# Residual stream kept token-major in a two-layer decoder trunk: down, w_out and wo with stationary activations, norms taken per token tile ahead of transposes

## The chip, the cores and the metric

One core of one Trainium2 chip runs the whole trunk. TensorE (PE) does the matmuls and its weight loads (PEld) run beside them; VectorE (DVE), ScalarE (ACT) and GpSimd (POOL) do the elementwise work; SyncE (SP) issues nearly all DMAs. Each engine works through its own list of instructions in a fixed order that a scheduler made when the kernel was built. The metric is device time in microseconds, from the first to the last instruction of the core plus what lies around them.

## The reference

512 tokens, width 1024, two layers, all in float32:

```python
for l in range(2):
    x = x + 0.5 * swiglu_ffn(rmsnorm(x, ffn1_norm[l]), gate, up, down)      # 1024 -> 2816 -> 1024
    z = rmsnorm(x, mix_norm[l]) @ w_in[l]                                    # 384 | 256 | 384 | 384 columns
    y = concat(s5(z_ssm), pool(z_pool), conv_module(z_v, z_g))
    x = x + y @ w_out[l]
    x = x + cross_attention(rmsnorm(x, xattn_norm[l]), rmsnorm(mem, mem_norm[l]), wq, wk, wv, wo)
    x = x + 0.5 * swiglu_ffn(rmsnorm(x, ffn2_norm[l]), gate, up, down)
return rmsnorm(x, final_norm)
```

rmsnorm(x, g) is x * rsqrt(mean(x^2) + 1e-6) * g. The conv module is v * sigmoid(g), a causal depthwise convolution of 31 taps, a layer norm over its 384 channels, and silu.

## The kernel before

**Layout.** The residual stream is feature-major: eight tiles `xs[k]` of 128 features by 512 tokens. Every projection has its weights stationary (128 x 128) and the activations of all 512 tokens moving, so its output is feature-major again. x is transposed on PE when it is loaded, and once more in the last FFN, whose last block is computed with stationary activations to give token-major output rows.

**Precision.** Weights and activations are split into two float32r parts, and `mm3` (L236 to L238) does three passes for each product. `wload` fetches a weight tile (L225), ACT makes the high part (L227), DVE or POOL the low part (L229); pools of three buffers stage them.

**Norms.** `Norm.add(k)` is called as soon as feature tile k of the residual stream is final: it splits x times gain, not yet divided by the root mean square, into `xh` and `xl`, and adds up squares. The next projections start on these at once. Meanwhile 4 matmuls against ones sum the squares over features (`ss_`, L202), DVE, POOL and PE turn that into a row factor that is broadcast over partitions (`pb_`, L214, copied to `rb` on ACT), and each projection multiplies by `rb` when its PSUM tile is evacuated on DVE: L269 and L273 in the FFN, L569, L572, L585 and L602 in the mixer, L853 in the attention.

**FFN.** 22 blocks of 128 hidden features; `gate_up(f)` makes one, and `down(p)` folds a group of six or five into the stream, eight output tiles each. `bg` is background work of the first phases (parameters, the memory's norm, the S5 matrices `s5_build`).

**Mixer.** In the order of PE: `pool_in` (`pp`), `conv_in(0)` (`pv`, `pgt`), `ssm_in` (`psu`), the other `conv_in`, then the keys and values of the memory (`kps`, `vps`), the S5 scan (`sps`, `yps`, `gps`) and w_out (`po`). On DVE stand the scaled memory `mg` (L800), the gated conv input `ch` (L569 to L573), the S5 input `su` (L585), then 3 x 29 multiply-adds of the convolution (`cacc`, L727) with S5 steps (`sy`, `sys`) between them, and the sum `lsm` that starts the layer norm (`lmean`, L740). The first half of w_out fills PE while the layer norm runs.

**Attention.** Per head: `q_proj` (`qps`), `scores`, softmax, and one head later `out_head` (`pv_`). After the last `out_head`, `wo` is applied to all eight feature tiles (`pwo`).

**Tail.** `finish` computes the last block token tile by token tile: residual add (L320), squares with an accumulator (L322), mean (L326), power on POOL (L327), scaling (L332, L334) and the output DMA.

Of the kernel before, what the change touches and what calls it, by code (L numbers as in the profile page):

```python
# [17 lines left out]
P = 128  # L18
# [26 lines left out]
def trunk_kernel(ctx: ExitStack, tc: tile.TileContext, io, out, phases=None):  # L45
# [30 lines left out]
    bp = ctx.enter_context(tc.tile_pool(name="bp", bufs=36))  # L76
# [86 lines left out]
    load_vecs(0)  # L163

# [6 lines left out]
    class Norm:  # L171
        def __init__(self, name, col, sum_eng=V):
            self.name, self.col, self.sum_eng = name, col, sum_eng
            self.xg = [None] * NK
            self.acc = None

        def sums(self, kt):
            sq = bt(f"sq_{self.name}{kt}")
            A.activation(out=sq, in_=xs[kt], func=AF.Square)
            if self.acc is None:  # L180
                self.acc = sq
            else:
# [10 lines left out]
        def r4(self):  # L193
            return rsqrt_cols(self.acc, 1.0 / D, self.name)
# [60 lines left out]
    def ffn(which, l, norm, nxt, bg):  # L255
# [22 lines left out]
        def down(p):  # L278
            f0, n = starts[p], sizes[p]
            last = p == len(sizes) - 1  # L280
            for o in range(NK):
# [3 lines left out]
                if last:  # L285
                    nxt.add(o)
# [736 lines left out]
```

## Time and profile before

| | |
|---|---|
| median of 3 runs | 2139.57 us (2138.98 to 2139.76) |
| span of the profiled execution | 2138.3 us |
| median less that span | 1.3 us |
| PE busy | 2088.5 us, 98% of the span |
| PEld busy | 1733.4 us, 81% |
| DVE busy | 1301.8 us, 61% |
| ACT busy | 751.5 us, 35% |
| POOL busy | 441.7 us, 21% |
| DMA queue q1, share of 16 engines | 33.8% |

The time of the profiled execution itself was not listed, so its span stands for it; the median lies 1.3 us above that span. A share is an average over the whole program: what a stage is worth is read from its own windows.

### The profile page before, as it was taken

The page shows a single profiled execution, that of the slowest core. Times are in us where ns is not written, and L with a number is a line of the kernel's source. Part 1 is how long each engine was busy: PE and PEld are TensorE (multiplying, and loading weights), DVE is VectorE, ACT ScalarE, POOL GpSimd, SP SyncE. Part 2 cuts the span into 40 slices and gives each one's busy share as a digit, 9 for nine tenths or more (in the row PEclk, how much of TensorE's full clock was granted, in tenths as well). Part 3 has the DMA queues.
Part 4 walks back from the last instruction along what each step waited for, and adds up shares of the span by engine and source line. Part 5 has one row for each costly group of instructions (what it writes and reads, how often), then busy time and mean ns, then how long its engine had stood idle before and what let it go on. Part 6 is the DMA issues. An engine that isn't in the chain of part 4 may idle for free.

```text
span 2138.3 us, 25180 instructions
## 1 busy us (share of the span) xinstructions
PE 2088.5 (98%) x9685; PEld 1733.4 (81%) x9685; DVE 1301.8 (61%) x1942; ACT 751.5 (35%) x1060; POOL 441.7 (21%) x477
## 2 busy tenths in 40 slices
PE   8999999989999999999999999999989999999998
PEld 6888888877787888888887888887868878888887
DVE  7766454699755544444577564456996655454454
ACT  4423222434434322222352323233344443222232
POOL 2217170457000000000013680006550000000000
PEclk9999999989999999999999999999999999999999
DMA  5342332444322323333333333334443323333241
GB/s 168 98 125 75 115 98 73 133 125 132 98 80 58 91 85 112 88 94 105 89 95 93 104 96 99 103 89 128 125 124 89 89 59 94 94 96 101 80 147 40
DMA packets 396256, 213.03 MB, mean 100 GB/s; under 512 B 31934, under 2 KB 387048, under 8 KB 396136
## 3 DMA queue, kind: packets, MB, share of 16 engines
q1 hardware_dynamic: 395344, 210.32, 33.8%
q8 instruction: 76, 1.25, 0.3%
q10 hardware_dynamic: 792, 1.10, 0.1%
q14 instruction: 44, 0.36, 0.1%
HBM read 203.32 MB, written 6.29 MB: 98 GB/s over the span
## 4 chain that ended last, share of the span: by engine, by line
PE 86%; DVE 10%; issue 1%; DMA 1%; ACT 1%; SPq 0%; POOL 0%; POOLq 0%; DVEq 0%; ACTq 0%
PE pgffn L236 7%; PE pgffn L237 7%; PE pgffn L238 7%; PE puffn L237 7%; PE puffn L238 7%; PE puffn L236 7%; PE pdffn L238 7%; PE pdffn L236 7%; PE pdffn L237 7%; DVE cacc L727 3%; PE qps L237 1%; PE po L236 1%; PE qps L236 1%; PE po L238 1%; PE pwo L236 1%
## 5 line engine op out<-in xcount | busy, mean ns | idle before, releaser
L236 PE MATMUL pgffn<-xh_ffn,wh_gffn 128*128 128x512 f32 x696 | 272.6, 392 | 0.0
L237 PE MATMUL puffn<-xl_ffn,wh_uffn 128*128 128x512 f32 x696 | 272.2, 391 | 0.0
L238 PE MATMUL puffn<-xh_ffn,wl_uffn 128*128 128x512 f32 x696 | 271.9, 391 | 0.0
L236 PE MATMUL puffn<-xh_ffn,wh_uffn 128*128 128x512 f32 x696 | 271.6, 390 | 0.0
L237 PE MATMUL pgffn<-xl_ffn,wh_gffn 128*128 128x512 f32 x696 | 271.4, 390 | 0.0
L238 PE MATMUL pgffn<-xh_ffn,wl_gffn 128*128 128x512 f32 x696 | 271.3, 390 | 0.0
L238 PE MATMUL pdffn<-h_ffffn,wl_dffn 128*128 128x512 f32 x664 | 257.9, 389 | 0.9 <-DVE wl_dffn L229 0.9
L237 PE MATMUL pdffn<-l_ffffn,wh_dffn 128*128 128x512 f32 x664 | 258.3, 389 | 0.0
L236 PE MATMUL pdffn<-h_ffffn,wh_dffn 128*128 128x512 f32 x664 | 257.8, 389 | 0.0
L227 ACT ACTIVATE wh_dffn<-wr_dffn 128x768 fp32r<-128x768 f32 (+1 forms) x120 | 94.9, 795 | 286.9 <-PE pdffn L237 148.3
L284 DVE SCALAR_TENSOR_TENSOR x<-pdffn,x 128x512 f32<-128x512 f32 x120 | 82.4, 689 | 168.7 <-PE pdffn L238 168.6
L273 DVE TENSOR_TENSOR uffn<-puffn,rb_ffn 128x512 f32<-128x512 f32 x88 | 60.7, 690 | 197.8 <-PE puffn L238 197.8
L227 ACT ACTIVATE wh_uffn<-wr_uffn 128x1024 fp32r<-128x1024 f32 x87 | 92.2, 1060 | 250.7 <-PE pgffn L237 155.2
L227 ACT ACTIVATE wh_gffn<-wr_gffn 128x1024 fp32r<-128x1024 f32 x87 | 92.2, 1060 | 249.5 <-issue 154.7
L269 DVE TENSOR_TENSOR affn<-pgffn,rb_ffn 128x512 f32<-128x512 f32 x88 | 60.7, 690 | 164.8 <-PE pgffn L238 158.6
L236 PEld LDWEIGHTS puffn<-xh_ffn,wh_uffn 128*128 128x128 f32 x696 | 131.0, 188 | 27.4 <-issue 0.2
L237 PEld LDWEIGHTS puffn<-xl_ffn,wh_uffn 128*128 128x128 f32 x696 | 131.0, 188 | 27.5 <-issue 0.2
L238 PEld LDWEIGHTS puffn<-xh_ffn,wl_uffn 128*128 128x128 f32 x696 | 131.0, 188 | 27.0
L238 PEld LDWEIGHTS pgffn<-xh_ffn,wl_gffn 128*128 128x128 f32 x696 | 130.7, 188 | 27.3
L237 PEld LDWEIGHTS pgffn<-xl_ffn,wh_gffn 128*128 128x128 f32 x696 | 130.8, 188 | 26.6
L236 PEld LDWEIGHTS pgffn<-xh_ffn,wh_gffn 128*128 128x128 f32 x696 | 130.7, 188 | 26.5
L238 PEld LDWEIGHTS pdffn<-h_ffffn,wl_dffn 128*128 128x128 f32 x664 | 124.6, 188 | 27.2 <-DVE wl_dffn L229 1.3
(456 smaller groups left out, 4197.4 us busy)
## 6 DMA issues: line engine op xcount, KB each, us to landing
wr_gffn<-in_ffn_w_gate_dram SPq DMA_DIRECT2D x87, 512.0 KB
wr_uffn<-in_ffn_w_up_dram SPq DMA_DIRECT2D x87, 512.0 KB
wr_dffn<-in_ffn_w_down_dram SPq DMA_DIRECT2D x64, 384.0 KB
wr_dffn<-in_ffn_w_down_dram SPq DMA_DIRECT2D x56, 320.0 KB
wr_k<-in_xattn_wk_dram SPq DMA_DIRECT2D x16, 512.0 KB
wr_v<-in_xattn_wv_dram SPq DMA_DIRECT2D x16, 512.0 KB
wr_wo<-in_w_out_dram SPq DMA_DIRECT2D x16, 512.0 KB
wr_q<-in_xattn_wq_dram SPq DMA_DIRECT2D x16, 512.0 KB
```

The source lines that it names most:

```text
L227: A.activation(out=h, in_=raw, func=AF.Copy)
L236: T.matmul(ps, lhsT=wh, rhs=ah, start=first, stop=False)
L237: T.matmul(ps, lhsT=wh, rhs=al, start=False, stop=False)
L238: T.matmul(ps, lhsT=wl, rhs=ah, start=False, stop=last)
L269: V.tensor_tensor(out=a, in0=pg, in1=rb, op=MUL)
L273: V.tensor_tensor(out=u, in0=pu, in1=rb, op=MUL)
L284: V.scalar_tensor_tensor(out=xs[o], in0=ps, scalar=0.5, in1=xs[o], op0=MUL, op1=ADD)
L727: V.scalar_tensor_tensor(out=acc[:, d:], in0=h[:, 0:S - d], scalar=cw[:, TAPS - 1 - d:TAPS - d], in1=acc[:, d:], op0=MUL, op1=ADD)
```

## The change

The residual stream becomes four token tiles `xt[t]` of 128 tokens by 1024 features, loaded by plain row DMAs. `down`, w_out and wo swap operands: 128 x 128 pieces of the activations are stationary, and rows of the weight matrix, 512 columns at a time, are moving, so their output is token-major and is added to `xt` by `add_x`. Each norm works per token tile: `Norm.half` squares each half (ACT, with an accumulator), and after the second half DVE, POOL and DVE make the normalised row tile `xn` with the gain, which is loaded broadcast over all partitions (`gb`); 8 PE transposes bring it feature-major, ACT copies `xh` and DVE makes `xl`. The projections then need no row factor. The first projection after a norm goes through `proj_halves`, two passes over 256 tokens each, so that its first half needs only token tiles 0 and 1. The FFN groups become 6, 6, 6, 4, and the last group's weight rows are kept in SBUF so that `finish` goes token tile by token tile in every FFN; w_out and wo do the same with their last three and two row blocks. Some evacuations go to ACT (`su`, `pd`), sigmoids read PSUM directly, and the first pass of wo (three heads) is placed ahead of the last head's `out_head`.

```diff
     class Norm:
...
+        def half(self, t, h):
...
+            A.activation(out=sq, in_=xt[t][:, dsl(h)], func=AF.Square, scale=D ** -0.5, accum_out=ss[:, h:h + 1])
+            if h == 1:
+                V.tensor_scalar(out=ss[:, 2:3], in0=ss[:, 0:1], scalar1=ss[:, 1:2], scalar2=EPS, op0=ADD, op1=ADD)
+                G.tensor_tensor(out=ss[:, 3:4], in0=ss[:, 2:3], in1=nhalf[:, 0:1], op=ALU.pow)
+                for i in range(2):
+                    self.emit(t, i, ss[:, 3:4])
+
+        def emit(self, t, h, r):
+            xn = bt(f"xn_{self.name}{t}{h}")
+            V.scalar_tensor_tensor(out=xn, in0=xt[t][:, dsl(h)], scalar=r, in1=self.gb[h], op0=MUL, op1=MUL)
+            ps = ax(f"xp_{self.name}{t}{h}", (P, NK // 2, P))
+            for k in range(NK // 2):
+                T.transpose(ps[:, k, :], xn[:, k * P:(k + 1) * P], ident)
+            A.activation(out=self.hl[0][h][:, :, tsl(t)], in_=ps, func=AF.Copy)
+            V.tensor_tensor(out=self.hl[1][h][:, :, tsl(t)], in0=ps, in1=self.hl[0][h][:, :, tsl(t)].bitcast(F32), op=SUB)
...
+    def proj_halves(items, acts):
+
+        n = len(acts)
+        for c in range(2):
+            cs = slice(c * S // 2, (c + 1) * S // 2)
+            for ps, (h, lo) in items:
+                for k, (ah, al) in enumerate(acts):
+                    mm3(ps[:, cs], h[:, k, :], lo[:, k, :], ah[:, cs], al[:, cs], c == 0 and k == 0, k == n - 1, True)
+
+
+    def rows_pass(dst, w, k0, acts, dh, name, first, last, eng=None, marks=None):
...
+            with tc.issue_after(marks[j // 2]) if marks else nullcontext():
+                for t, ps in dst:
+                    for i in range(m):
+                        ah, al = acts[j + i]
+                        mm3(ps, ah[:, tsl(t)], al[:, tsl(t)], got[j + i][0], got[j + i][1], first and j + i == 0,
+                            last and j + i == n - 1)
+        return got
...
+        def finish():
             for t in range(NT):
...
+                for dh in range(2):
+                    ps = mm(f"pl{which}{l}_{t}{dh}")
+                    rows_kept(ps, t, [gs[fl + i] for i in range(nl)], [kept[i][dh] for i in range(nl)], True, True)
+                    add_x(t, dh, ps, 0.5)
+                    nxt.half(t, dh)
...
-            a = vt(f"ca{l}_{i}")
-            V.tensor_tensor(out=a, in0=pgt, in1=rb, op=MUL)
-            A.activation(out=a, in_=a, func=AF.Sigmoid)
             h = vt(f"ch{l}_{i}")
-            V.tensor_tensor(out=h, in0=pv, in1=rb, op=MUL)
-            V.tensor_tensor(out=h, in0=h, in1=a, op=MUL)
+            A.activation(out=h, in_=pgt, func=AF.Sigmoid)
+            V.tensor_tensor(out=h, in0=pv, in1=h, op=MUL)
...
-            V.tensor_tensor(out=u, in0=pu.rearrange("p (c j) -> p j c", j=CH), in1=rbp, op=MUL)
+            A.activation(out=u, in_=pu.rearrange("p (c j) -> p j c", j=CH), func=AF.Copy)
...
+        n1 = (NH - 1) * HD // P
+        first = {(t, 0): (mm if t < 3 else cx)(f"pwo{l}_{t}0") for t in range(NT)}
+        rows_pass([(t, first[t, 0]) for t in range(NT)], wo, 0, os_[:n1], 0, f"xo{l}", True, False)
         out_head(NH - 1)
```

On DVE, the start of the convolution in layer 0's mixer reads as follows before the change: `mg` are the eight low parts of the scaled memory, `ca` and `ch` the gate and the value of conv tile 0, `su` the S5 input.

```order
L800 SCALAR_TENSOR_TENSOR mg_3_3493<-mn_1_3488,pcols_322,mg_3_3493 128x256
L569 TENSOR_TENSOR ca_0_3474<-pgt_0_3443,rb_mix_3344 128x512
L572 TENSOR_TENSOR ch_0_3477<-pv_0_3412,rb_mix_3344 128x512
L573 TENSOR_TENSOR ch_0_3477<-ch_0_3477,ca_0_3474 128x512
L800 SCALAR_TENSOR_TENSOR mg_4_3498<-mn_2_3496,pcols_322,mg_4_3498 128x256
L800 SCALAR_TENSOR_TENSOR mg_5_3501<-mn_2_3496,pcols_322,mg_5_3501 128x256
L727 SCALAR_TENSOR_TENSOR cacc_0_4464<-ch_0_3477,convw,cacc_0_4464 128x510
L727 SCALAR_TENSOR_TENSOR cacc_0_4464<-ch_0_3477,convw,cacc_0_4464 128x509
L800 SCALAR_TENSOR_TENSOR mg_6_3506<-mn_3_3504,pcols_322,mg_6_3506 128x256
L800 SCALAR_TENSOR_TENSOR mg_7_3509<-mn_3_3504,pcols_322,mg_7_3509 128x256
L727 SCALAR_TENSOR_TENSOR cacc_0_4464<-ch_0_3477,convw,cacc_0_4464 128x508
L585 TENSOR_TENSOR su_0_3583<-psu_0_3552,rb_mix_3344 128x512
```

The same place on DVE after the change (`pq` is the pooled mean of pool tile 0, whose sums `pw` POOL makes):

```order
L801 SCALAR_TENSOR_TENSOR mg_4_3471<-mn_2_3469,pcols_344,mg_4_3471 128x256
L801 SCALAR_TENSOR_TENSOR mg_5_3474<-mn_2_3469,pcols_344,mg_5_3474 128x256
L801 SCALAR_TENSOR_TENSOR mg_6_3479<-mn_3_3477,pcols_344,mg_6_3479 128x256
L801 SCALAR_TENSOR_TENSOR mg_7_3482<-mn_3_3477,pcols_344,mg_7_3482 128x256
L584 TENSOR_TENSOR ch_0_3450<-pv_0_3388,ch_0_3450 128x512
L630 TENSOR_TENSOR pq_0_3492<-pw_0_2_3488,inv_0_106 128x16
L632 SCALAR_TENSOR_TENSOR pq_0_3492<-pw_0_2_3488,inv_0_106,pd_0_3384 128x496
L631 TENSOR_TENSOR pq_0_3492<-pq_0_3492,pd_0_3384 128x16
L737 SCALAR_TENSOR_TENSOR cacc_0_4431<-ch_0_3450,convw,cacc_0_4431 128x510
L737 SCALAR_TENSOR_TENSOR cacc_0_4431<-ch_0_3450,convw,cacc_0_4431 128x509
```

All eight `mg` now stand ahead of `ch_0`, which is one instruction instead of three, `su` is gone from DVE, and `pq_0` stands between `ch_0` and the first tap.

On PE, the first projection of layer 0's mixer before the change, around the sum of squares (`xh_mix` and `xl_mix` are the eight feature tiles, `wh_pl` and `wl_pl` the weights of the pool group):

```order
L237 MATMUL pp_0_3346<-xl_mix_3325,wh_pl_0_3349 128x512
L238 MATMUL pp_0_3346<-xh_mix_3323,wl_pl_0_3351 128x512
L238 MATMUL pp_1_3379<-xh_mix_3173,wl_pl_1_3384 128x512
L202 MATMUL ss_mix_3330<-ones_92,sq_mix_3118 128x1 x4
L236 MATMUL pp_1_3379<-xh_mix_3203,wh_pl_1_3382 128x512
L237 MATMUL pp_1_3379<-xl_mix_3205,wh_pl_1_3382 128x512
```

The same projection on PE after the change, where the first half (tokens 0 to 255) ends and the second begins (`xp_mix` are the transposes of the two halves of token tile 3):

```order
L250 MATMUL pp_1_3275<-xh_mix_3059,wh_pl_1_3284 128x256
L251 MATMUL pp_1_3275<-xl_mix_3061,wh_pl_1_3284 128x256
L252 MATMUL pp_1_3275<-xh_mix_3059,wl_pl_1_3286 128x256
L200 MATMUL xp_mix_3258<-ident,xn_mix_3256 128x128 x4
L200 MATMUL xp_mix_3267<-ident,xn_mix_3265 128x128 x4
L250 MATMUL pp_0_3274<-xh_mix_3058,wh_pl_0_3278 128x256
L250 MATMUL pp_1_3275<-xh_mix_3058,wh_pl_1_3284 128x256
L250 MATMUL pv_0_3388<-xh_mix_3058,wh_v_0_3391 128x512
L251 MATMUL pp_0_3274<-xl_mix_3060,wh_pl_0_3278 128x256
L252 MATMUL pp_0_3274<-xh_mix_3058,wl_pl_0_3280 128x256
```

The sum of squares has left PE; the eight transposes of the last token tile stand directly ahead of the second half, which reads their result.

## Rows read from the trace of the kernel before

**Rows 1.** The page, first part: busy time, share and instructions of each engine.
```profile
PE 2088.5 (98%) x9685; PEld 1733.4 (81%) x9685; DVE 1301.8 (61%) x1942; ACT 751.5 (35%) x1060; POOL 441.7 (21%) x477
```

**Rows 2.** Windows; columns PE, PEld, DVE, ACT, POOL busy (count), PE clock, DMA, GB/s.
```profile
380.00:400.00 20.00, 20.00 (x94) 16.71 (x93) 14.25 (x18) 11.00 (x15) 8.39 (x4) 1.00 0.49 141
416.25:545.85 129.60, 117.06 (x616) 97.75 (x614) 124.25 (x173) 50.33 (x68) 78.11 (x46) 0.92 0.43 126
1471.68:1601.18 129.50, 115.26 (x616) 96.63 (x614) 123.73 (x173) 51.02 (x68) 78.22 (x46) 0.95 0.43 127
```

**Rows 3.** Waits of PE, the whole span.
```profile
PE yps L681 <- DVE sy L677: 10.9, 4, 4.1
PE gps L706 <- DVE sys L696: 10.7, 4, 3.9
PE pv_30a L236 <- ACT pth L891: 1.5, 2, 0.8
```

**Rows 4.** Timeline of PE around a norm's sum of squares.
```profile
398.45 0.95 PE L202 MATMUL ss_mix<-ones,sq_mix 128*128 128x1 f32 x8
399.26 0.49 PE L236 MATMUL pp<-xh_mix,wh_pl 128*128 128x512 f32 x1
```

**Rows 5.** Timeline of PE in the memory's keys, first and last of eleven matmuls.
```profile
499.05 0.28 PE L237 MATMUL kps<-mg,wh_k 128*128 128x256 f32 x1
...
500.25 0.28 PE L238 MATMUL kps<-mg,wl_k 128*128 128x256 f32 x1
```

**Rows 6.** Timeline of PE around eight of the last FFN's transposes.
```profile
2067.92 0.40 PE L238 MATMUL puffn<-xh_ffn,wl_uffn 128*128 128x512 f32 x1
2068.15 1.04 PE L296 MATMUL xtp<-ident,x 128*128 128x128 f32 x8
2068.95 0.48 PE L236 MATMUL pgffn<-xh_ffn,wh_gffn 128*128 128x512 f32 x1
2069.26 0.40 PE L237 MATMUL pgffn<-xl_ffn,wh_gffn 128*128 128x512 f32 x1
```

**Rows 7.** Groups by line on PE, 2066 to 2071 us.
```profile
L296 PE MATMUL xtp<-ident,x 128*128 128x128 f32 x8 | 1.0, 273 | 0.0
```

**Rows 8.** Timeline of the tail, behind the last matmul.
```profile
2131.78 0.69 DVE L320 SCALAR_TENSOR_TENSOR xt<-pl,xt 128x512 f32<-128x512 f32 x1 [1.98 <-PE pl L238]
2132.51 0.63 ACT L322 ACTIVATE fsq<-xt 128x512 f32<-128x512 f32 x1 [2.67 <-DVE xt L320]
...
2133.26 0.21 DVE L326 TENSOR_SCALAR fss<-fss 128x1 f32<-128x1 f32 x1
2133.62 0.54 POOL L327 TENSOR_TENSOR fss<-fss,nhalf 128x1 f32<-128x1 f32 x1 [6.26 <-DVE fss L326]
2134.20 0.48 DVE L334 TENSOR_SCALAR xt<-fg,fss 128x512 f32<-128x512 f32 x1 [0.72 <-POOL fss L327]
```

**Rows 9.** Groups by line on DVE, 416.25 to 545.97 us.
```profile
L573 DVE TENSOR_TENSOR ch<-ch,ca 128x512 f32<-128x512 f32 x3 | 4.9, 1634 | 0.1
L800 DVE SCALAR_TENSOR_TENSOR mg<-mn,pcols,mg 128x256 fp32r<-128x256 f32 x4 | 4.8, 1238 | 0.0
L585 DVE TENSOR_TENSOR su<-psu,rb_mix 128x512 f32<-128x512 f32 x3 | 3.4, 1134 | 0.0
L572 DVE TENSOR_TENSOR ch<-pv,rb_mix 128x512 f32<-128x512 f32 x2 | 1.3, 670 | 0.0
```

**Rows 10.** Timeline of all engines at the first ch.
```profile
415.77 2.41 POOL L229 TENSOR_TENSOR wl_su<-wr_su,wh_su 128x1024 fp32r<-128x1024 f32 x1 [3.06 <-ACT wh_su L227]
...
416.25 2.48 DVE L573 TENSOR_TENSOR ch<-ch,ca 128x512 f32<-128x512 f32 x1
```

**Rows 11.** The page, fifth part: out<-in xcount, busy us, mean ns, idle before.
```profile
L273 DVE TENSOR_TENSOR uffn<-puffn,rb_ffn 128x512 f32<-128x512 f32 x88 | 60.7, 690 | 197.8 <-PE puffn L238 197.8
```

**Rows 12.** Timeline of PE at the start.
```profile
15.40 0.78 PE L236 MATMUL pgffn<-xh_ffn,wh_first_gate 128*128 128x512 f32 x1
```

More of the change, by code (lines that the diff above doesn't have):

```diff
@@ new lines, in prep, with take @@
+        def prep(self):
+            self.gb = [bt(f"gb_{self.name}{h}") for h in range(2)]
+            for h in range(2):
+                nc.sync.dma_start(out=self.gb[h], in_=self.gain[dsl(h)].partition_broadcast(P))
+            self.take()
+        def take(self):
+            hl = [[xgp.tile([P, NK // 2, S], F32R, tag=f"x{z}", name=f"x{z}_{self.name}{h}") for h in range(2)]
+                  for z in "hl"]
+            self.hl = hl
+            self.xg = [(hl[0][k // 4][:, k % 4, :], hl[1][k // 4][:, k % 4, :]) for k in range(NK)]
@@ new lines, in rows_kept, with add_x @@
+    def rows_kept(ps, t, acts, kept, first, last):
+        n = len(acts)
+        for i, ((ah, al), (wh, wl)) in enumerate(zip(acts, kept)):
+            mm3(ps, ah[:, tsl(t)], al[:, tsl(t)], wh, wl, first and i == 0, last and i == n - 1)
+    def add_x(t, dh, ps, scale=None):
+        x_ = xt[t][:, dsl(dh)]
+        if scale is None:
+            V.tensor_tensor(out=x_, in0=ps, in1=x_, op=ADD)
+        else:
+            V.scalar_tensor_tensor(out=x_, in0=ps, scalar=scale, in1=x_, op0=MUL, op1=ADD)
@@ L255, in ffn @@
     def ffn(which, l, norm, nxt, bg):
         wg, wu, wd = (io[f"{which}_w_{n}"][l] for n in ("gate", "up", "down"))
-        rb = norm.rb()
-        sizes = [6, 6, 5, 5]
-        starts = [0, 6, 12, 17]
+        sizes = [6, 6, 6, 4]
+        starts = [sum(sizes[:i]) for i in range(len(sizes))]
         gs = {}
@@ L274, in gate_up @@
-            V.tensor_tensor(out=a, in0=a, in1=s, op=MUL)
-            V.tensor_tensor(out=a, in0=a, in1=u, op=MUL)
-            gs[f] = split(a, f"ff{nm}")
+            ps = [mm(f"p{z}{nm}") for z in "gu"]
+            w = [pre.pop(n, None) or wcols(w_, 0, NK, f * P, f"{n[0]}{nm}") for n, w_ in (("gate", wg), ("up", wu))]
+            if f == 0:
+                proj_halves(list(zip(ps, w)), norm.xg)
+            else:
+                for z in range(2):
+                    proj(ps[z], None, 0, 0, norm.xg, None, split_w=w[z])
@@ L342, in ffn @@
                     down(p - 1)
-                if nxt is None and f0 == fl:
-                    if i == 0:
-                        for h in range(2):
-                            gain.append(st(f"fgain{h}"))
-                            nc.sync.dma_start(out=gain[h], in_=io["final_norm"][h * 512:(h + 1) * 512].partition_broadcast(P))
-                    else:
-                        to_tokens(i - 1)
-                    fetch_rows(i)
+                if f0 == fl:
+                    kept.append(keep_rows(wd, fl + i, f"last{which}{l}_{i}", st if i < 3 else vc))
                 next(bg, None)
```

278 lines of the change are left out of this document (119 added, 159 removed).

## The prediction

> **What bounds the kernel now.** The page's first part comes first: PE is busy 98% of the span and every other engine at most 61%, apart from PE's own weight loads [rows 1]. So the time is the number of PE passes times their spacing, plus the places where PE stops. The windows say where it stops: an FFN stretch shows PE busy 20.00 of 20 us at full clock, and the large hole is in the two mixers [rows 2]. Between the first gated conv input (ch) and the sum that opens the layer norm (lsm), 129.60 us in layer 0, PE is busy 117.06 and its mean clock is 0.92; DVE is busy 124.25, 96%. Layer 1 repeats it, with 115.26 and 123.73. PE waits there for DVE's S5 results, 10.9 and 10.7 us over the two layers [rows 3]. In this stretch DVE is the bound: idle PE (12.5 us) and the time at the lower clock (8% of 129.6, 10 us, some of it idle too) come to about 20 us a layer that PE doesn't need.
>
> The reader should therefore see three kinds of place: FFN, where only PE passes count; the mixer stretch, where only DVE work counts; and the seams at each norm, where at present nothing is lost.
>
> **PE passes.** The products are the same in number; swapping which operand is stationary changes no count of 128x512 passes in down, w_out and wo. Three things differ.
> - Transposes go from 64 (x on load, and the last FFN) to 256 (eight norms, 32 each): 192 more. Eight of them take from 2068.15 to 2068.95, 0.80 us, and the matmul behind them takes 0.31 to the next start instead of the 0.23 of the one ahead [rows 6], so 0.88 for eight. 24 eights: +21.1. If groups of four each pay that 0.08, up to +2 more.
> - The first projection of each norm in halves: 8 norms x 2 tiles x 24 passes = 384 passes of 512 columns become 768 of 256. Eleven 256-column matmuls stand 1.20 us from first to last, 0.12 each [rows 5], against 0.23 for 512 columns [rows 6]: 384 x (0.24 - 0.23) = +3.8.
> - The sum of squares (0.81 us from 398.45 to 399.26 [rows 4]) and the broadcast, which I price alike because it is eight passes too, go away at eight norms: 16 x 0.89 with the same 0.08 = -14.2.
> Sum **+11**, bounds 8 and 15.
>
> The row of the group says 273 ns for a mean transpose [rows 7], but that is a latency: eight overlap and cost 0.80 together [rows 6]. The Trainium skill (TensorE: Matmul & The Clock Gate, "Part 4: PE-mode transpose") gives some 275 ns in one kernel's context; by it 192 would cost 53 us instead of 21. The durations of this trace agree with that figure, the spacing does not bear it out as a price.
>
> **The mixers.** Of DVE's work in the stretch [rows 9], the row-factor multiplies go: L569 and L572 with two each inside it (1.3 each by the row of L572; L569 is its like), and the three su (3.4) move to ACT, which is busy only 50.33 of 129.60 there [rows 2]. The four mg that lay inside (4.8) are now ahead of ch. The multiply of gate and value, L573, costs 4.9 for three; in its place comes one that reads PSUM, like L572, at 0.67 each, 2.0. Total 1.3 + 1.3 + 3.4 + 4.8 + 2.9 = 13.7 a layer at most, well under the 20 us that PE can give.
>
> The 2.48 us of the first L573 fall together with a POOL subtraction of 2.41 us that began just ahead [rows 10], while L572, with PSUM as one input, takes 0.67 [rows 9]. The Trainium skill (SBUF — State Buffer, "Who interferes with whom") says that a DVE instruction with two SBUF inputs contends with a GpSimd instruction that reads SBUF and one with a single SBUF input doesn't; the trace agrees, and by it the 2.9 us are a true saving.
>
> I don't take the whole 13.7. The savings all lie at the front of the stretch, where the taps of conv tiles 1 and 2 still wait for their projections on PE, and pq, which needs POOL's sums, now stands ahead of the first tap; if POOL is late, 87 taps queue behind it. At the low end only the su (3.4) count, about 4. I take 9.5, nearer the full sum since DVE is 96% busy all along: **-19** for two layers, bounds -8 and -27.
>
> **The seams.** At seven norms (all but the first) the projection now needs the normalised tokens. From the last matmul of token tile 3 the chain is that of the tail [rows 8]: residual add at 2131.78 until the factor is used at 2134.20, 2.4 us; then the scaling to xn (0.69, like L320), four transposes (0.4), the copy to xh (0.6, like the squares), the subtraction to xl (0.7): 4.8 us for the first half and 5.5 for the second. Cover: the first halves of the projection, 48 x 0.12 = 5.8, and the eight transposes of tile 2, 0.8. That would hide it, but the transposes of tile 3 stand directly ahead of the second halves, so copy and subtraction (1.3 us) stay exposed save for the matmuls that need only xh. I take 0.85 each, **+6**, bounds 2 and 12. If the cover were gone a seam would cost 5.5. On DVE, tile 3's adds and scalings queue behind tile 2's xl and weight subtractions, so any delay there comes on top.
>
> **The start.** Before, the first matmul starts at 15.40 [rows 12] and works from feature tiles as they come. Now token tiles need the whole chain of 4.8 us, four times, on a DVE that does per tile the two scalings, two subtractions and a mean: 4 x 0.69 + 0.21, 3.0 us. The four take 12 us, so the second half of the tokens is ready some 10 us behind the first matmul, with only 5.8 us of first halves to fill it; part comes back because no load transposes and no copies of x stand ahead. I take **+2.5**, bounds -2 and +6.
>
> **Attention and tail.** Three heads of wo go ahead of the last out_head, which covers its wait for probabilities, 1.5 us over two layers [rows 3]: **-1.5**, bounds 0 and -3. At the end the two halves of the last scaling stood on ACT and DVE side by side (0.48 on DVE); now both are on DVE at 0.69: **+0.6**.
>
> **At nothing.** The FFN loses two DVE multiplies of 60.7 us each (L269 is L273's like), but DVE sat idle 197.8 us ahead of L273 waiting for PE [rows 11]; PE hides them. Evacuations of down are as many as before, four PSUM tiles finishing in a row with 1.4 us (six passes) between them against 0.69 a piece. The gain rows are two more DMAs a norm, with the DMA engines under half busy in the windows [rows 2].
>
> **Sum.** 11 - 19 + 6 + 2.5 - 1.5 + 0.6 = -0.4 on a span of 2138.3: 2137.9; the median of the runs shown lies 1.3 above that span, so **2139 us**. A difference below 0.2%, 4.3 us, can't be told from none here.
>
> **The rivals.**
> 1. Faster, about 2129. DVE gives the full 13 a layer (-26) and the seams cost 0.4 each (3): 11 - 26 + 3 + 2.5 - 1.5 + 0.6 = -10.4. For it: DVE's 96% and the 20 us that PE has to give. Against: the late conv inputs. Chance 0.31.
> 2. Slower, by the seams, about 2159. DVE is 71% busy in the FFN stretch [rows 2], and with adds, scalings and xl of one tile per 5.5 us of PE it gets fuller; if two weight subtractions (1024 columns, so 1.4 each by the 0.69 for 512) stand ahead of tile 3's scaling, a seam grows by 2.8 and seven by 20. It decides once the chain passes its 6.6 us of cover by more than about 1.5 us on average. Chance 0.14.
> 3. Slower, by the mixers, about 2150. The DVE saving turns into waits for POOL's sums or conv projections and only 4 a layer remain (-8). For it: pq's new place. Chance 0.13.
> 4. Slower, about 2170: transposes cost their latency, 192 x (0.273 - 0.110) = +31. It is what the skill's figure as a price would give. Against: the spacing of rows 6. Chance 0.03.
>
> Another 0.03 is left for a stall that I don't see (kept rows waiting for buffers of the S5 preparation in layer 0, say). The forecast itself, no change, gets 0.36.
>
> **Range and chances.** The forecast's own range is 2135 to 2144. For 8 in 10 it reaches to most of rival 1 below, 2126, and takes in rival 3 and part of rival 2 above, 2154. Faster 0.31, same 0.36, slower 0.33.
>
> **What would show it.** The stretch from ch to lsm should shrink from 129.6 to about 120 us in both layers, with DVE still above 90%. Transposes in groups of four should be about 0.1 us apart. At each seam PE should show one or two gaps, of 0.85 us together, whose releaser is ACT's xh or DVE's xl. The first 48 FFN passes should end some 2.5 us later. The prediction is wrong if the stretch stays above 125, if DVE waits for POOL ahead of the first tap, or if seams cost over 1.5 us each; and in the other direction if the seams show no gaps.

## The result, and the profile after

The changed kernel takes 2152.05 us (2149.74 to 2154.13, 4 runs) against 2139.28 us before: ratio 1.0057, 95% interval 1.0042 to 1.0071, so 12.8 us slower. That lies inside the forecast's range (2126 to 2154), near its upper end, but no change was forecast. The profiled execution has a span of 2152.3 us; it is the slowest of the four (2154.13 us), so the stage times below run some 2 us above the median.

The page's first part, to be set beside [rows 1]: DVE has 147 us less to do, and PE is busy for 14.5 us more.

```profile
PE 2103.0 (98%) x10132; PEld 1765.3 (82%) x10132; DVE 1154.4 (54%) x1743; ACT 724.4 (34%) x1105; POOL 426.3 (20%) x496
```

The time in which PE is idle, span less busy, is 49.8 us before and 49.3 after. What the mixers gave back was spent again at new waits, and the passes came on top.

Where the time went is seen from the starts of a few first matmuls on PE's timeline, in both kernels. The last column shares the prediction's terms out over the stages (a transpose at 0.11, a halved projection at 0.5, sum of squares and broadcast together at -1.8, a seam at 0.85, and so on).

| stage, from first matmul to first matmul (us) | before | after | change | by the terms |
|---|---|---|---|---|
| start to pool_in, layer 0 (one FFN) | 390.97 | 397.99 | +7.0 | +3.0 |
| pool_in to lmean, layer 0 | 155.00 | 148.92 | -6.1 | -8.2 |
| lmean to q of head 0, layer 0 | 46.39 | 51.67 | +5.3 | +1.8 |
| attention, layer 0 | 119.31 | 126.41 | +7.1 | +2.3 |
| two FFNs between | 734.73 | 737.03 | +2.3 | +6.1 |
| pool_in to lmean, layer 1 | 154.93 | 146.26 | -8.7 | -8.2 |
| lmean to q of head 0, layer 1 | 46.38 | 49.68 | +3.3 | +1.8 |
| attention, layer 1 | 119.35 | 125.19 | +5.8 | +2.3 |
| last FFN and tail | 371.26 | 369.20 | -2.1 | -1.6 |

The mixers came out near their terms, although the one of layer 0 holds a new wait of 5.2 us for lsm. The start stands 4 us above its term, the attentions 8 and the stages behind lmean 5; the two FFNs between stand 4 below theirs.

PE's waits over the whole span answer to [rows 3]; the columns are us in total, times, longest. The S5 waits (yps, gps) fell from 21.6 to 8.6 us; new are those of the transposes (xp) for DVE, of lmean for lsm, and a longer one of the last head (pv_30a).

```profile
PE xp_ffn L200 <- DVE xn_ffn L197: 10.5, 1, 10.5
PE yps L691 <- DVE sy L687: 5.9, 3, 2.5
PE lmean L750 <- DVE lsm L748: 5.4, 2, 5.2
PE xp_ffn L200 <- DVE xl_ffn L202: 4.9, 4, 2.6
PE xp_att L200 <- DVE xl_att L202: 4.8, 2, 2.4
PE pv_30a L250 <- DVE ptl L895: 4.3, 2, 2.1
PE gps L716 <- DVE sys L706: 2.7, 1, 2.7
...
PE pgffn L250 <- ACT xh_ffn L201: 0.5, 2, 0.2
...
PE pp L250 <- ACT xh_mix L201: 0.3, 1, 0.3
```

**The mixers.** Windows from ch to lsm, layers 0 and 1, with the columns of [rows 2]:

```profile
424.95:546.85 121.90, 111.97 (x614) 95.64 (x612) 117.97 (x163) 50.68 (x68) 75.93 (x42) 0.96 0.41 124
1488.63:1608.23 119.60, 115.61 (x614) 98.57 (x612) 113.75 (x161) 48.26 (x64) 71.26 (x40) 0.93 0.41 123
```

The stretch went from 129.6 to 121.9 and 119.6 us, as forecast, and DVE is still 95% to 97% busy.

**The seam into the attention**, layer 0, on the timeline of DVE and PE. `x` is the add of token tile 3, `wl_q` the low part of the second head's weights:

```profile
597.66 1.41 DVE L197 SCALAR_TENSOR_TENSOR xn_att<-x,ss_att,gb_att 128x512 f32<-128x512 f32 x2
...
598.58 0.50 PE L250 MATMUL qps<-xh_att,wh_q 128*128 128x256 f32 x2 [0.41 <-ACT xh_att L201]
598.99 0.68 DVE L315 TENSOR_TENSOR x<-po,x 128x512 f32<-128x512 f32 x1
599.59 1.22 DVE L243 TENSOR_TENSOR wl_q<-wr_q,wh_q 128x1024 fp32r<-128x1024 f32 x1
...
600.72 1.28 DVE L202 TENSOR_TENSOR xl_att<-xp_att,xh_att 128x512 fp32r<-128x512 f32 x2
601.46 1.11 PE L200 MATMUL xp_att<-ident,xn_att 128*128 128x128 f32 x4 [2.38 <-DVE xl_att L202]
```

The transposes of token tile 2 wait 2.38 us, and not for their own input xn, which was ready at 599.1, but for tile 1's xl: the kernel gives the transposes two PSUM buffers, and xl is the last to read one. Three kinds of work stand ahead of that xl on DVE (the two xn of tile 2, the add, the weight subtraction), and all but two matmuls of the first halves of the projection are queued behind the transposes on PE. The cover that the prediction counted on was there, but behind the instruction that waits.

**The last head**, layer 0, on the timeline:

```profile
688.38 1.04 PE L893 MATMUL pt<-ident,e 128*128 128x128 f32 x8
688.58 1.06 ACT L241 ACTIVATE wh_xo<-wr_xo 128x1024 fp32r<-128x1024 f32 x1 [4.39 <-PE pwo L252]
689.54 1.06 ACT L894 ACTIVATE pth<-pt 128x512 fp32r<-128x512 f32 x2
689.67 1.23 DVE L243 TENSOR_TENSOR wl_xo<-wr_xo,wh_xo 128x1024 fp32r<-128x1024 f32 x1 [4.22 <-ACT wh_xo L241]
690.81 1.28 DVE L895 TENSOR_TENSOR ptl<-pt,pth 128x512 fp32r<-128x512 f32 x2
...
691.55 0.50 PE L250 MATMUL pv_30a<-pth,vh 128*128 128x512 f32 x1 [2.13 <-DVE ptl L895]
```

wo's first pass did go ahead of the last head, but all of it stands ahead of the transposes of the probabilities (`pt`). Between these and the matmuls that use them PE has nothing to do, and a weight copy on ACT and a weight subtraction on DVE stand there in the queues. The wait grew from 1.5 to 4.3 us over two layers. In return the waits of heads 1 and 2 (pv_10a, pv_20a), 2.1 us over two layers before, are gone.

**The sum that opens the layer norm**, layer 0, on the timelines of POOL and DVE:

```profile
541.02 6.96 POOL L243 TENSOR_TENSOR wl_wo<-wr_wo,wh_wo 128x1024 fp32r<-128x1024 f32 x3 [2.72 <-ACT wh_wo L241]
```

```profile
541.91 2.20 DVE L746 TENSOR_TENSOR lsm<-cv,cv 128x512 f32<-128x512 f32 x1
544.14 2.71 DVE L748 TENSOR_TENSOR lsm<-lsm,cv 128x512 f32<-128x512 f32 x1
```

Two sums that take 0.68 us each in layer 1 take 4.9 together, beside three subtractions on POOL. PE waits 5.2 us.

**The clock behind the new waits.** Windows of PE (busy, clock, DMA, GB/s): behind the wait for lsm, behind layer 0's seam into the attention, behind layer 1's, and behind the last heads of layers 0 and 1:

```profile
546.91:553.00 6.09, 6.09 (x12) 0.50 0.41 129
602.00:604.20 2.20, 2.20 (x12) 0.50 0.69 200
1660.84:1664.25 3.41, 3.41 (x29) 1.00 0.56 159
692.99:696.41 3.42, 3.42 (x9) 0.50 0.75 245
1751.12:1754.54 3.42, 3.42 (x9) 0.50 0.77 253
```

The granted clock is 0.50, the lower of the two levels (1.2 GHz), for 6.1 us behind lsm, for at least 2.2 us behind layer 0's seam and for 3.4 us behind each last head. At half clock the work takes twice as long (nine matmuls in the 3.4 us), so that is 3.0, 1.1 and twice 1.7 us more, 7.5 in all. Layer 1's seam has the same wait of 2.38 us and the full clock behind it. Nor does a last head's wait always bring the lower clock: in x8 (below) PE waits the same 2.13 us there and runs on at 1.00, 15 matmuls in 3.4 us.

```profile
689.84:693.26 3.42, 3.42 (x15) 1.00 0.74 208
```

**The start**, on PE's timeline:

```profile
10.49 1.97 PE L200 MATMUL xp_ffn<-ident,xn_ffn 128*128 128x128 f32 x8 [10.49 <-DVE xn_ffn L197]
15.10 1.97 PE L200 MATMUL xp_ffn<-ident,xn_ffn 128*128 128x128 f32 x8 [2.64 <-DVE xl_ffn L202]
...
20.12 0.41 PE L252 MATMUL pgffn<-xh_ffn,wl_first_gate 128*128 128x256 f32 x1
20.33 0.41 PE L250 MATMUL pgffn<-xh_ffn,wh_first_gate 128*128 128x256 f32 x1
```

The pattern is that of the seam (transposes behind xl; a third such wait, of 1.29 us, follows at 18.99). The first half passes stand 0.21 us apart instead of the 0.12 of [rows 5], so at some half the pace; the profile's windows give no lower granted clock for them, so what slowed them is not shown.

**The gift.** Before, PE also waited in layer 1's first FFN for a DMA of an S5 parameter, by this row of its waits; after, no such wait is left:

```profile
PE cps L474 <- DMA cn<-in_ssm_c_im_dram: 2.2, 1, 2.2
```

Behind that wait the kernel before ran at the lower clock, by a window of PE:

```profile
1139.27:1142.69 3.42, 3.42 (x11) 0.50 0.32 86
```

So it cost 2.2 us and 1.7 at half clock, 3.9 together, about the 3.8 us by which the two FFNs between came out below their terms. The prediction had no term for it, and why the wait is gone was not looked into.

### The profile page after: what moved, and what is told of

It reads as the page before. It is cut to its first block, busy times and chain, and to the rows that moved or that the text cites. A ratio compares the mean times of both kernels' runs of the same rounds, so it can differ in the third digit from the quotient of the medians.

```text
span 2152.3 us, 25954 instructions
## 1 busy us (share of the span) xinstructions
PE 2103.0 (98%) x10132; PEld 1765.3 (82%) x10132; DVE 1154.4 (54%) x1743; ACT 724.4 (34%) x1105; POOL 426.3 (20%) x496
## 3 DMA queue, kind: packets, MB, share of 16 engines
q8 instruction: 79, 1.29, 0.2%
## 4 chain that ended last, share of the span: by engine, by line
PE 89%; DVE 6%; ACT 1%; DMA 1%; issue 1%; POOL 0%; SPq 0%; DVEq 0%; POOLq 0%; ACTq 0%
PE pgffn L250 7%; PE pgffn L251 7%; PE pgffn L252 7%; PE puffn L252 7%; PE puffn L250 7%; PE puffn L251 7%; PE pdffn L250 6%; PE pdffn L252 6%; PE pdffn L251 6%; DVE cacc L737 1%; PE qps L251 1%; PE qps L252 1%; PE qps L250 1%; PE pwo L250 1%; PE pwo L251 1%; PE pwo L252 1%
## 5 line engine op out<-in xcount | busy, mean ns | idle before, releaser
L250 PE MATMUL pgffn<-xh_ffn,wh_gffn 128*128 128x512 f32 (+1 forms) x720 | 277.1, 385 | 0.6 <-ACT xh_ffn L201 0.5
L251 PE MATMUL pgffn<-xl_ffn,wh_gffn 128*128 128x512 f32 (+1 forms) x720 | 276.5, 384 | 0.0
L250 PE MATMUL puffn<-xh_ffn,wh_uffn 128*128 128x512 f32 (+1 forms) x720 | 275.5, 383 | 0.0
L251 PE MATMUL puffn<-xl_ffn,wh_uffn 128*128 128x512 f32 (+1 forms) x720 | 275.5, 383 | 0.0
L252 PE MATMUL puffn<-xh_ffn,wl_uffn 128*128 128x512 f32 (+1 forms) x720 | 275.4, 382 | 0.0
L252 PE MATMUL pgffn<-xh_ffn,wl_gffn 128*128 128x512 f32 (+1 forms) x720 | 275.3, 382 | 0.0
L251 PE MATMUL pdffn<-wl_dffn,h_ffffn 128*128 128x512 f32 x576 | 224.2, 389 | 0.0
L252 PE MATMUL pdffn<-wh_dffn,l_ffffn 128*128 128x512 f32 x576 | 224.2, 389 | 0.0
L250 PE MATMUL pdffn<-wh_dffn,h_ffffn 128*128 128x512 f32 x576 | 223.7, 389 | 0.5 <-DVE sffn L337 0.5
L243 DVE TENSOR_TENSOR wl_gffn<-wr_gffn,wh_gffn 128x1024 fp32r<-128x1024 f32 x87 | 115.6, 1329 | 49.8 <-ACT wh_gffn L241 49.6
```

The costliest lines, as they stand in the source:

```text
L243: (eng or V).tensor_tensor(out=lo, in0=raw, in1=h.bitcast(F32), op=SUB)
L250: T.matmul(ps, lhsT=wh, rhs=ah, start=first, stop=False, skip_group_check=skip)
L251: T.matmul(ps, lhsT=wh, rhs=al, start=False, stop=False, skip_group_check=skip)
L252: T.matmul(ps, lhsT=wl, rhs=ah, start=False, stop=last, skip_group_check=skip)
```

## The experiments

All are edits of the changed kernel. The kernel before was at 2140.08 us on the chip of the first four, 2139.54 on that of the next four, 2139.61 on that of x9 to x11 and 2138.76 for x13. The changed kernel's own ratio to it, with which the ratios below compare, is 1.0057 (1.0042 to 1.0071).

**x1, the second head's query weights on POOL.**
```diff
-            ws = [wcols(wq, 0, NK, hd * HD + dh * P, f"q{l}_{hd}{dh}") for dh in range(2)]
+            ws = [wcols(wq, 0, NK, hd * HD + dh * P, f"q{l}_{hd}{dh}", G if hd == 1 else V) for dh in range(2)]
```


> The changed kernel, with only the low parts of the second head's query weights (two 1024-column subtractions a layer) made on POOL instead of DVE. Theory A (the seam into attention is held by DVE's queue: a weight subtraction of 1.2 us and what it displaces stand ahead of the xl that PE waits 2.4 us for): that wait falls under 0.8 us in both layers, the half-clock matmuls behind it go too, the attention stages shrink by 2 to 3 us each, and the whole is 4 to 6 us below the changed kernel's 2152.1, about 2147. Theory B (the norm chain itself is too long, whatever stands beside it): the wait moves to the next transposes or the next xl and the time stays within 1 us of 2152.

Measured: 2153.73 us, ratio 1.0067 (1.0053 to 1.0080). The wait grew, from 4.8 to 6.7 us. The timeline says why:
```profile
595.50 2.45 POOL L243 TENSOR_TENSOR wl_q<-wr_q,wh_q 128x1024 fp32r<-128x1024 f32 x1 [0.74 <-ACT wh_q L241]
595.66 3.50 DVE L197 SCALAR_TENSOR_TENSOR xn_att<-x,ss_att,gb_att 128x512 f32<-128x512 f32 x2
```
The subtraction left DVE's queue, but while POOL reads SBUF the two xn, which read both x and the gain from SBUF, take 3.50 instead of 1.41 us. So this run does not decide between queue and chain: it exchanged one delay for another. The Trainium skill (SBUF — State Buffer, "Who interferes with whom") has this contention for DVE instructions with two SBUF inputs; the trace agrees.

**x2, wo's first pass on POOL.**
```diff
-        rows_pass([(t, first[t, 0]) for t in range(NT)], wo, 0, os_[:n1], 0, f"xo{l}", True, False)
+        rows_pass([(t, first[t, 0]) for t in range(NT)], wo, 0, os_[:n1], 0, f"xo{l}", True, False, G)
```


> The changed kernel, with only the low parts of wo's first pass (three subtractions a layer) made on POOL instead of DVE. Theory A (the last head's value matmuls wait 2.1 us a layer because a weight subtraction of wo's first pass stands ahead of ptl on DVE): that wait falls under 1 us and the time is 3 to 5 us below 2152.1. Theory B (the wait is that of the softmax chain, DVE's queue adds nothing): the wait keeps its 2 us and the time stays within 1 us; if POOL's 2.4 us a piece come too late for wo's own matmuls, it rises by 1 to 3 us.

Measured: 2154.58 us, ratio 1.0071 (1.0059 to 1.0084); the wait stayed at 4.4 us. The subtraction ahead of ptl was still there: it belongs to wo's second pass. The edit missed its mark, and x6 repeats it in the right place.

**x3, w_out's first pass on DVE instead of POOL.**
```diff
-        rows_pass([(t, first[t, 0]) for t in range(NT)], w_out, 0, ys[:n1], 0, f"wo{l}", True, False, G,
+        rows_pass([(t, first[t, 0]) for t in range(NT)], w_out, 0, ys[:n1], 0, f"wo{l}", True, False, V,
```


> The changed kernel, with only the low parts of w_out's first pass (three subtractions a layer) made on DVE instead of POOL. Theory A (in layer 0 the two sums of lsm took 2.2 and 2.7 us instead of 0.68 because POOL's 2.4 us subtractions ran beside them, and PE waited 5.2 us for lsm): both sums take about 0.7, the wait for lsm falls to 3 us or less in spite of a subtraction of 1.2 us between them, and the time falls by 1 to 3 us. Theory B (lsm is late because DVE has too much work ahead of it): the wait stays at 5 us or grows by the 1.2 us, time 0 to 3 us up.

Measured: 2150.7 us, ratio 1.0042 (1.0030 to 1.0055). Both sums are back at 0.7 us, and the wait for lsm fell from 5.4 to 3.3 us. The layer norm's next step (ss_ln waiting for lsq), however, went from 0.7 to 2.4 us. The direction is as theory A has it, the whole is not clear of the changed kernel's interval.

**x4, every transpose twice.**
```diff
+            for k in range(NK // 2):
+                T.transpose(ps[:, k, :], xn[:, k * P:(k + 1) * P], ident)
```


> The changed kernel with every one of the 256 transposes of the norms done twice (the second writes the same values to the same place). If a transpose costs its spacing, 0.10 us, as the prediction took it, the time rises by 256 x 0.10 to 0.11 = 26 to 28 us, plus up to 5 us where transposes stand on a waited-for chain: about 2180. If it costs its latency of 0.273 us, it rises by 70 us, to 2222.

Measured, in one run: 2172.18 us, 20 us above the changed kernel, where 26 to 28 or 70 were expected. On the timeline the second set starts 0.44 us behind the first, four transposes at 0.11:
```profile
727.15 0.60 PE L202 MATMUL xp_ffn<-ident,xn_ffn 128*128 128x128 f32 x4
727.59 0.60 PE L200 MATMUL xp_ffn<-ident,xn_ffn 128*128 128x128 f32 x4
```
The latency as a price is out. The price by spacing is the nearer one, but 6 to 8 us of it did not show. PE's idle time is no smaller (49.6 us against 49.3), so where they went is open; the mean granted clock was 0.992 in this profile and 0.989 in that of the changed kernel.

**x5, xl ahead of the next xn at every norm.**
```diff
-            V.scalar_tensor_tensor(out=xn, in0=xt[t][:, dsl(h)], scalar=r, in1=self.gb[h], op0=MUL, op1=MUL)
+            with tc.issue_after(self.prev) if t and h == 0 else nullcontext():
+                V.scalar_tensor_tensor(out=xn, in0=xt[t][:, dsl(h)], scalar=r, in1=self.gb[h], op0=MUL, op1=MUL)
...
-            ws = [wcols(wq, 0, NK, hd * HD + dh * P, f"q{l}_{hd}{dh}") for dh in range(2)]
+            with tc.issue_after(norm.prev) if hd == 1 else nullcontext():
+                ws = [wcols(wq, 0, NK, hd * HD + dh * P, f"q{l}_{hd}{dh}") for dh in range(2)]
```
(`prev` is the last xl of the tile before; `issue_after` queues what stands under it behind that instruction.) 

> The changed kernel with DVE's order alone edited: the scaling xn of a token tile is queued behind the xl of the tile before it, at every norm, and the second head's query weight subtractions behind the last xl. Nothing moves to another engine. Theory A (PE's transposes wait because a PSUM buffer of two is freed only by xl, and on DVE the next tile's xn, the next add and a weight subtraction stand ahead of that xl): the 2.4 us waits at the two seams into attention fall under 1 us, at the start the waits for xl of 4.9 us in all halve, and the time falls by 5 to 9 us, to about 2145. Theory B (the chain of a token tile is simply longer than what PE has to do, the order on DVE only chooses which link is late): the waits move to xn or to the later tiles and the time stays within 1.5 us of 2152.

Measured: 2157.21 us, ratio 1.0083 (1.0069 to 1.0097). In the attentions theory A holds: no wait of a transpose for xl_att is left, and the stages take 122.7 and 122.8 us instead of 126.4 and 125.2. At the start, in layer 0's seam into the mixer and at lsm it comes out worse; these are its waits:
```profile
PE xp_ffn L201 <- DVE xn_ffn L198: 17.3, 4, 10.3
PE lmean L752 <- DVE lsm L750: 10.2, 2, 5.2
...
PE xp_att L201 <- DVE xn_att L198: 0.7, 2, 0.4
```
At the start the transposes now wait 6.6 us for xn beyond the first 10.3, where they had waited 4.7 for xl; this is what theory B has. And lsm meets POOL in layer 1 too. Which link is late is decided by the order of the queues, seam by seam. Three PSUM buffers in place of two were not tried.

**x6, wo's second pass on POOL.**
```diff
-        w1 = rows_pass([(0, first[0, 1])], wo, 0, os_[:n1], 1, f"xo{l}", True, False)
+        w1 = rows_pass([(0, first[0, 1])], wo, 0, os_[:n1], 1, f"xo{l}", True, False, G)
```


> The changed kernel with only the low parts of wo's second pass (token tile 0, columns 512 to 1023; three subtractions a layer) on POOL. These, not those of the first pass, were the ones ahead of ptl on DVE. Theory A: the wait of the last head's value matmuls, 2.1 us a layer, falls to about 1 us (copy pth 0.6 and half a subtraction are left), time 2 to 3 us down. Theory B (the wait is ACT's, with its weight copy ahead of pth): it falls by less than 0.5 us a layer and the time stays within 1 us.

Measured: 2150.48 us, ratio 1.0044 (1.0030 to 1.0058). The wait fell to 1.5 us a layer, between the two theories' figures. The attention stages took 124.5 and 122.9 us, 1.9 and 2.3 less than in the changed kernel; but in x8, whose edit lies at the start, they took 125.1 each, so not all of that is the edit's.
```profile
PE pv_30a L250 <- DVE ptl L895: 3.0, 2, 1.5
```

**x7, the first projections in whole passes.**
```diff
-            if f == 0:
-                proj_halves(list(zip(ps, w)), norm.xg)
-            else:
+            if True:
                 for z in range(2):
```
(and alike in pool_in and q_proj.) 

> The changed kernel with the first projection after each norm done in whole 512-column passes again, so that its first matmul needs all four token tiles. Theory A (the halves are the cover of the norm chain): 384 passes give back 4 to 5 us, but each of seven seams and the start now shows 4 to 5.5 us of wait before its first projection, some 30 to 40 us, so 2177 to 2187. Theory B (the halves cover little, since PE waits at the second half anyway): the time falls by 2 to 5 us.

Measured: 2197.48 us, ratio 1.0270 (1.0256 to 1.0284), 45 us above the changed kernel and more than theory A has. Of its waits:
```profile
PE xp_ffn L200 <- DVE xn_ffn L197: 22.1, 4, 10.4
```
The halves are the cover; without them the seams show their chain. PE is idle 32 us longer (81.4 against 49.3), about what theory A has, and its mean granted clock is 0.981 instead of 0.989, which the theory left out.

**x8, the first token tile ahead of the gain rows.**
```diff
-    cur.prep()
     for t in range(NT):
         nc.sync.dma_start(out=xt[t], in_=x_d[tsl(t), :])
+        if t == 0:
+            cur.prep()
```


> The changed kernel with the first token tile's DMA issued ahead of the two broadcast gain rows instead of behind them. Theory A (the start is late because x lands behind the gain rows, and each link of the chain follows): the first transposes come 1 to 1.5 us earlier (10.5 before), full-speed matmuls begin 1 to 2 us earlier, time 1 to 3 us down. Theory B (DVE's queue sets the start): the first transposes come earlier and the first whole stretch of matmuls does not, time within 1 us.

Measured: 2150.58 us, ratio 1.0054 (1.0042 to 1.0067): not clear of the changed kernel. The first transposes came at 7.5 instead of 10.5 us and pool_in began 0.9 us earlier. So 3 us at the head of the chain were worth 1. The rest came back as waits at tokens 256 to 511, and behind ACT's queue rather than DVE's:
```profile
23.10 0.63 ACT L965 ACTIVATE msq<-ml 128x512 f32<-128x512 f32 x1 [4.75 <-DMA ml<-in_mem_dram]
23.73 1.06 ACT L201 ACTIVATE xh_ffn<-xp_ffn 128x512 fp32r<-128x512 f32 x2
```
```profile
27.31 0.38 PE L250 MATMUL pgffn<-xh_ffn,wh_first_gate 128*128 128x256 f32 x1 [0.98 <-ACT xh_ffn L201]
...
29.36 0.39 PE L251 MATMUL pgffn<-xl_ffn,wh_first_gate 128*128 128x256 f32 x1 [1.31 <-DVE xl_ffn L202]
```
`msq` squares the memory (`ml`) for its norm, as background work. It stands on ACT ahead of the xh of token tile 2 and waits for its DMA until 23.1, in the changed kernel until 23.04; DVE idles 3.4 us for that xh. No run moved msq.

**x9, lsm clear of weight subtractions.** w_out's first pass on DVE, queued behind the second sum:
```diff
-                V.tensor_tensor(out=sm, in0=sm, in1=cvs[i], op=ADD)
+                sm_ins = V.tensor_tensor(out=sm, in0=sm, in1=cvs[i], op=ADD).ins
...
+            with tc.issue_after(behind) if behind else nullcontext():
...
-                  (mark[0], mark[1], mark[1]))
+                  (mark[0], mark[1], mark[1]), sm_ins)
```


> The changed kernel with the low parts of w_out's first pass on DVE and queued there behind the second sum of lsm, so that nothing stands between the two sums and POOL doesn't read SBUF for w_out beside them. Theory A (in layer 0 POOL's subtractions stretch lsm, PE waits 5.2 us for it and then runs 6 us at half clock): both sums take 0.7 us, the wait in layer 0 falls to about 2 us, the stretch behind lmean runs at full clock, and the time falls by 4 to 6 us, to about 2147; layer 1, where lsm was not stretched, changes by less than 1 us. Theory B (PE is early, lsm is no later than its inputs): the wait stays above 4 us and the time within 1.5 us of 2152, or 1 to 2 us above, because two subtractions now stand ahead of the subtraction of the mean on DVE.

Measured: 2152.11 us, ratio 1.0056 (1.0043 to 1.0069): no change. Its sums and waits:
```profile
542.60 0.72 DVE L747 TENSOR_TENSOR lsm<-cv,cv 128x512 f32<-128x512 f32 x1
543.35 0.69 DVE L749 TENSOR_TENSOR lsm<-lsm,cv 128x512 f32<-128x512 f32 x1
```
```profile
PE ss_ln L216 <- DVE lsq L760: 3.6, 2, 2.4
```
In layer 0 the sums are short and lmean comes 3.2 us earlier after pool_in (145.7 instead of 148.9), as theory A has it. But the subtractions of 1.2 us now stand ahead of the layer norm's own work on DVE, ss_ln waits, and the stage behind lmean in layer 1 takes 54.4 instead of 49.7 us: 1.7 more of waiting for lsq, and some 3.4 from a stretch of 6.8 us at the lower clock behind it.
```profile
1612.37:1619.20 6.83, 6.83 (x21) 0.50 0.29 77
```
The contention is real; removing it by way of DVE's queue gave the gain back in this profile.

**x10, four edits together** (x9's, x5's at the attention alone, x6's and x8's). 

> The changed kernel with four edits together: x9's; DVE's order xl ahead of the next xn at the attention's norm alone, with the second head's query weight subtractions behind the last xl; the low parts of wo's second pass on POOL; the first token tile's DMA ahead of the gain rows. If the waits that these removed one by one add up (attention seam about 6 us in both layers together, last head 3, start 1.5, lsm 4), about 2138, level with the kernel before. If they are one and the same slack, so that each only passes on to the next, no less than 2146.

Measured: 2146.82 us, ratio 1.0030 (1.0018 to 1.0043). The attentions take 122.1 us each, but the first FFN, from its first projection matmul to pool_in, 384.8 instead of 381.1, and the stage behind lmean in layer 1 again 54.4. The gains of single edits do not add up.

**x11, su on DVE again.**
```diff
-            A.activation(out=u, in_=pu.rearrange("p (c j) -> p j c", j=CH), func=AF.Copy)
+            V.tensor_copy(out=u, in_=pu.rearrange("p (c j) -> p j c", j=CH))
```


> The changed kernel with the S5 input su copied out of PSUM on DVE again instead of ACT (three strided copies a layer, some 1.1 us each by the multiply that they were before). Theory A (DVE is the bound from ch to lsm, and what it is spared there comes back in full): the stretch, 121.9 and 119.6 us, grows by 3 to 3.5 us in each layer and the time by 5 to 7 us, to about 2158. Theory B (DVE's gain in the mixers went into waits, so the stretch is no longer DVE's): the stretch grows by less than 1 us and the time stays within 1.5 us.

Measured: 2154.91 us, ratio 1.0069 (1.0055 to 1.0084), not clear of the changed kernel. The copies take 0.68 us, not 1.1, and the stretches stayed:
```profile
424.56:546.64 122.08, 109.49 (x614) 92.46 (x612) 117.57 (x166) 49.03 (x65) 77.58 (x42) 0.97 0.43 126
1488.36:1607.38 119.02, 113.90 (x609) 98.02 (x608) 115.08 (x163) 46.33 (x60) 72.73 (x41) 0.93 0.43 127
```
Three instructions more, 2.05 us, and DVE's busy time in layer 0 is 0.4 us less: other instructions got shorter (the second lsm 1.63 instead of 2.71). By the stretch this is theory B's number, though DVE has no slack to show for it, being 96% busy. That the 2 us are lost in what collisions with POOL happen to cost is argued, not shown. Nor does the stretch tell all: in layer 1 an S5 step (`su`, 2.39 us) that stood ahead of the second lsm now stands behind it, and the stage behind lmean takes 54.0 instead of 49.7 us. By the time neither theory is decided.

**x13, the attention's edits alone** (x5's at the attention alone and x6's). 

> The changed kernel with only the attention's edits: at the attention's norm xl ahead of the next xn on DVE, the second head's query weight subtractions behind the last xl, and the low parts of wo's second pass on POOL. Start, FFN seams and mixers as in the changed kernel. Theory A (DVE's order in the attention stages is where 7 to 8 of the missing 14 us went): the two attention stages, 126.4 and 125.2 us, fall to about 122, as they did in the run with all edits, and the time to about 2145. Theory B (the waits only move on into the FFN seam or wo): the stages behind grow by what the attention loses and the time stays above 2149.

Measured: 2146.98 us (2145.77 to 2147.58), ratio 1.0031 (1.0019 to 1.0043). The attention stages take 122.1 us each, 4.3 and 3.1 us less, and the stages behind them did not grow: theory A. The profiled span of 2145.0 is 7.4 us below that of the changed kernel; by the medians the gain is 5.1. Of its waits:
```profile
PE xp_att L201 <- DVE xn_att L198: 0.7, 2, 0.4
```
Both its attention stages ran at a granted clock of 1.00. How much of the gain is that, layer 0 of x3 shows (its edit lies in the mixer): with waits of 2.02 us at the seam and 2.13 at the last head, but no lower clock, its attention took 123.2 us:
```profile
595.02:718.23 123.21, 118.50 (x640) 1.00 0.25 73
```
By this one profile the waits and the order alone are worth about 1 us of layer 0's 4.3, and the other 3 go with the lower clock that followed the waits in the changed kernel's profile. No kernel tried beats the one before.

## Why the prediction was wrong

**PE passes, right.** The spacing of transposes (0.11) is the price; the rival by latency is out (x4 rose by 20 us, where latency asks for 70).

**The mixers, right in size, and not what decided.** The stretch lost 7.7 and 9.9 us against 9.5. That each microsecond taken from DVE comes back was not shown: x11 put 2 back and the stretch did not move.

**The clock behind new waits: a term left out.** The prediction counted the lower clock in the mixers alone. In the changed kernel's profile it costs 7.5 us behind waits that the change brought or lengthened: 3.0 behind lsm, 1.1 behind layer 0's seam, 1.7 behind each last head. That is half of the miss. It does not come with each such wait (layer 1's seam, x3, x8), so it can't be read off a wait's length here.

**The seams, wrong by one step: "I take 0.85 each".** The total was near by luck, 7.7 us where +6 was taken: too much at five seams and too little at two. At the FFN and mixer seams the waits for xh and xl come to some 1.0 us in all, where five times 0.85 is 4.2. At the two seams into the attention there came 2.4 us of wait for xl and 0.4 for xh, in layer 0 also 1.1 at half clock: 3.9 and 2.8, past the 1.5 that the prediction named as a sign of being wrong. The step said that "any delay there comes on top" and priced it at nothing; rival 2 had the mechanism, weight subtractions in DVE's queue, but made seven seams pay it. The chain was taken as one of data alone. In its place the runs showed a PSUM buffer that xl frees, with DVE's order setting when (x5, x13). The prediction read the order of PE, at the mixer's seam, and never that of DVE.

**"Attention ... -1.5", wrong in sign.** The term counted the wait for the softmax that wo's first pass would hide. The wait from the probabilities' transposes to their use has no work of PE beside it and got longer by 2.8 us over two layers; half of that growth was a weight subtraction (x6). Against it stand the 2.1 us of heads 1 and 2, which had no term. Seam, last head and the lower clock behind them are what x13 gives back, 7.4 us by the profiles and 5.1 by the medians; its attention stages are 2.8 us longer than before, near the 2.3 of the terms.

**The start, mis-sized.** The stage to pool_in grew by 7.0 against 3.0. The sum had each tile's chain on DVE, not the order of the queues: xl frees the buffer late, as at the seam, and on ACT the memory's squares wait for their DMA ahead of an xh, which is where x8's gain went. Some 20 half passes at 0.21 instead of 0.12 us make 1.8 us more. The rest was not told apart.

**Not in the sum at all:** the step from lsm to lmean in layer 0, a wait of 5.2 us inside the mixer's stage and 3.0 at half clock behind it; 0.7 of wait for lsq in layer 1; and the gift of 3.9 us in layer 1's first FFN. Contention with POOL lengthened lsm (x3, x9); the gain of ending it was not got, since the work had to go somewhere on DVE.

The misses by the stage table: +4.0 at the start, +1.6 in the mixers to lmean, +5.0 behind lmean, +8.3 in the attentions, -3.8 in the FFNs, -0.5 at the end, 14.6 us together; the span grew by 14.0 where -0.4 was forecast, a miss of 14.4 (the 0.2 is rounding).

## What to carry to other kernels

When a chain of several engines is to be hidden behind a pass, count what is ahead of its last link in the queue of every engine on it, and who frees the buffer that its first link needs: cover that stands behind the waiting instruction on its own engine is no cover. A wait of PE can cost more than itself: here the lower clock that followed some of them added 7.5 us. A price found at one seam is not the price of the next, since the same code meets other neighbours there. Moving work off a busy engine onto one beside which it runs slower can cost as much as it saves (x1), and moving it back in front of another chain too (x9).

## What the runs showed of the hardware

Layer 0's mixer took 148.9, 151.2 and 151.2 us from pool_in to lmean in the profiles of the changed kernel, x2 and x6, whose edits lie in the attention. DVE and POOL worked through the same lists in the same order there, and single instructions took up to 2 us more or less; DVE was busy no longer in the longer ones, so the cause of the 2.3 us is open.

Two DVE sums of 0.68 us took 2.20 to 2.24 and 2.71 us beside POOL's subtractions in layer 0 of eight kernels' profiles (the changed kernel, x1, x2, x4, x5, x6, x8 and x13): such a collision can repeat to within 50 ns from kernel to kernel. In x11 the second sum took 1.63, and in x7 the second alone was long, 2.85.

In the changed kernel PE's wait of 5.2 us, one of its two waits of 2.4 and both of its waits of 2.1 were followed by microseconds at clock 0.50. The other wait of 2.4 was not, nor were the waits of 2.1 at the same place in x1, x3, x8 and x9.
